# Input projection: seven-product K pairs in fewer column chunks

## The chip, the cores and the metric

The kernel runs on one core of a Trainium2 chip. The metric is the device time of one execution in microseconds (us), lower is better. The core's engines work side by side, each through its own queue in order: PE (TensorE, matrix products), DVE (VectorE), ACT (ScalarE), POOL (GpSimd), and SP, which here only issues transfers.

## The reference

Two layers, 256 tokens, width 2048, all in float32. Each layer projects the normed input to twelve chunks of 512 columns, runs two kinds of attention on them, projects back, and adds a feed-forward block:

```python
h = rms_norm(x, pre_mix_norm[l])
proj = h @ w_in[l]              # (256, 2048) @ (2048, 6144)
# q, k, v of stick-breaking attention: column chunks 0 to 5
# q, k, v of differential attention: column chunks 6 to 11
x = x + rms_norm(mix @ w_o[l], post_mix_norm[l])
x = x + rms_norm(swiglu(rms_norm(x, pre_ffn_norm[l])), post_ffn_norm[l])
```

## The kernel before

**Products.** Each float32 factor is split into a rounded part and a rest (`hi` and `lo` for weights, two halves of `xT` for the input), and one product is three matmuls: hi times hi, hi times lo, lo times hi. ACT makes `hi`, DVE the rest `lo` (line 369). A matmul has 128 x 128 stationary values (input or attention data) and 512 moving ones (weights).

**Input projection** (`mixer_in`). The twelve column chunks are done in six pairs of chunks, in the order of `PAIRS`: (6, 8), (10, 7), (9, 0), (11, 2), (1, 3), (4, 5). They are called the first to sixth pair here, `n` is 0 to 5. The 2048 rows of K form eight *K pairs* of two blocks of 128 rows. For one K pair, two column chunks and two halves of the tokens, the plain way (`eight_in`) takes eight products, 24 matmuls. The other way (`phased`) takes seven products, 21 matmuls, by a scheme of the Strassen kind: it multiplies sums of weight blocks by sums of token blocks. The second to sixth pair do K pairs 0 to 3 (`IN_SEVEN`) in seven products and 4 to 7 (`IN_PLAIN`) in eight; the first pair does all eight plainly.

**What seven products need.** Sums of the weights are made on the way. A transfer engine adds two blocks in DRAM ahead of time (`sums_ahead`: a copy at line 302 and an adding transfer at line 308, both issued by POOL, into `sum`), and SP loads that into half of a `raw` tile; where the sum isn't ready when the order is written, DVE makes it (line 378). DVE then forms three more sums per K pair (lines 380, 384, 399, on `u` and `raw`), and seven halves of a `hi`/`lo` pair are split instead of four. In `phased`, all K pairs' first four products (g0, t1, t2, t3) come first; then ACT copies the four banks into `w` (`kept_part`, line 1222), DVE combines three of them (lines 1253 to 1255), and then come g1, b22 and t4. `settle` adds `w` to the banks at the end of the pair (line 1266). Sums of the token blocks are formed once per layer and K pair, and serve all pairs of chunks: `sums_of`, with `fin`, `sin`, `shin`, `slin` as tiles, called in the first pair at K pairs 3 to 6 (layer 0) or 2 to 5 (layer 1).

**Attention.** Its steps stand among the projection's matmuls. A `tick` is counted for every two products, and generators continue after so many ticks: `flip` transposes q and k (`qkT_ps`), `diff_weights` makes scores `s_df`, their softmax `e_df` (ACT) and its transposes `pT_df`, `attend` the outputs `o_df`; `stick_weights` uses `za_sb` and `zb_sb`. `rotate` turns q and k on POOL (lines 984 to 987).

**Order and room.** A scheduler puts the instructions of each engine in order ahead of time and may move one past another that it doesn't depend on. `hi` and `lo` have six buffers each, `raw` has four, and `feed_jobs` prepares weights a few tiles ahead of PE.

Of the kernel before, what the change touches and what calls it, by code (L numbers as in the profile page):

```python
# [22 lines left out]
KT = D // P  # L23
# [13 lines left out]
O_SEVEN = (4, 5)  # L37
PAIRS = ((6, 8), (10, 7), (9, 0), (11, 2), (1, 3), (4, 5))
IN_SEVEN = (0, 1, 2, 3)
IN_PLAIN = (4, 5, 6, 7)  # L40
SEVEN = (2, 4, 5, 6)
FIRST_SEVEN = (6,)
FIRST_ORDER = (0, 1, 3, 2, 7, 4, 6, 5)
# [37 lines left out]
def weight_order():  # L81

    order = []

    def queue(*blocks):
        order.append(blocks)
        return len(order) - 1

    def queue_pair(name, l, kp, c):
        return queue((name, l, 2 * kp, c), (name, l, 2 * kp + 1, c))  # L90

    roles = {}

    def queue_phase(key, name, l, kps, cc):
        for a, b in zip(kps[::2], kps[1::2]):
            roles[queue(*((name, l, 2 * kp + 1, cc[1]) for kp in (a, b)))] = "u1", key, (a, b)
            for kp in (a, b):
                roles[queue(*((name, l, 2 * kp, c) for c in cc))] = "first", key, (kp,)
        for a, b in zip(kps[::2], kps[1::2]):
            roles[queue(*((name, l, 2 * kp + 1, cc[0]) for kp in (a, b)))] = "g1", key, (a, b)  # L100

    plan = []
    sevens, own = set(), set()
    for l in range(L):
        lay = {"in": {}, "o": {}, "gate": {}, "up": {}, "down": {}}
        for n, (ca, cb) in enumerate(PAIRS):
            if n:
                queue_phase(("in", l, n), "w_in", l, IN_SEVEN, (ca, cb))
            for kp in IN_PLAIN if n else range(KT // 2):
                lay["in"][ca, kp] = queue_pair("w_in", l, kp, ca)  # L110
                lay["in"][cb, kp] = queue_pair("w_in", l, kp, cb)
        queue_phase(("o", l), "w_o", l, KP_O[:2], (0, 1))
        order_o = [(c, kp) for kp in KP_O[2:] for c in (0, 1)]
        order_o += [(c, kp) for kp in LATE_O for c in (2, 3)] + [(c, kp) for c in (2, 3) for kp in LAST_O]
        lay["order_o"] = order_o
        for c, kp in order_o:
            lay["o"][c, kp] = queue_pair("w_o", l, kp, c)
            if c == 3 and kp in O_SEVEN:
                own.add(lay["o"][c, kp])
        for c in range(FF // CW):  # L120
            for kp in gate_order(c):
                lay["gate"][c, kp] = queue_pair("w_gate", l, kp, c)
                lay["up"][c, kp] = queue_pair("w_up", l, kp, c)
                if kp in gate_sevens(c):
                    sevens.add(lay["up"][c, kp])
        for half in range(2):
            cc = (2 * half, 2 * half + 1)
            order_d = [(c, kp) for kp in range(FF // P // 2) for c in cc]
            if half == 1 and l + 1 < L:
                order_d[-len(DOWN_LATE) :] = DOWN_LATE  # L130
            for c, kp in order_d:
                lay["down"][c, kp] = queue_pair("w_down", l, kp, c)
                if c % 2 and kp in DOWN_SEVEN[half]:
                    sevens.add(lay["down"][c, kp])
        plan.append(lay)
    return order, plan, sevens, own, roles
# [49 lines left out]
def kernel(  # L186
# [802 lines left out]
    def opening(pool, accs, xT, stats, sums_of, settle):  # L989

        xr = []

        def load():
            kp = len(xr)
            xr.append(pool.tile([P, 2, S], F32, tag="tok", name=f"xr{kp}"))
            nc.sync.dma_start(xr[kp], x_columns[:, 2 * kp : 2 * kp + 2, :])

        opened = []

        def split(k):  # L1000
            g, src = gains[:, k : k + 1], xr[k // 2][:, k % 2, :]
            if k == 0:
                with tc.high_priority(offset=URGENT):
                    opened.append(nc.vector.tensor_scalar(out=xT[k][:, 0, :], in0=src, scalar1=g, scalar2=None, op0=ALU.mult))
            else:
                nc.scalar.activation(xT[k][:, 0, :], src, AF.Copy, scale=g)
            nc.vector.scalar_tensor_tensor(
                out=xT[k][:, 1, :], in0=src, scalar=g, in1=xT[k][:, 0, :].bitcast(F32), op0=ALU.mult, op1=ALU.subtract
            )

        xr.append(pool.tile([P, 2, S], F32, tag="tok", name="xr0"))
        nc.scalar.dma_start(gains[:, 0:32], gain_columns[:, 0:32])
        nc.scalar.dma_start(xr[0][:, 0, :], x_columns[:, 0, :])
        nc.scalar.dma_start(xr[0][:, 1, :], x_columns[:, 1, :])
        both = []
        for i in range(2):
            both.append((
                wpool.tile([P, 2, CW], F32, tag="raw", bufs=4, name=f"raw{i}"),
                wpool.tile([P, 2, CW], F32R, tag="hi", bufs=6, name=f"hi{i}"),
                wpool.tile([P, 2, CW], F32R, tag="lo", bufs=6, name=f"lo{i}"),  # L1020
            ))
            raws.append(both[i][0])
        for kk in range(2):
            for i in range(2):
                loads.append(nc.sync.dma_start(raws[i][:, kk, :], stream[i][:, kk, :]))
        load()
        fetch(4)
        for kk in range(2):
            split(kk)
            for raw, hi, lo in both:  # L1030
                nc.scalar.activation(hi[:, kk, :], raw[:, kk, :], AF.Copy)  # L1031
                with tc.issue_after(opened[0].ins):
                    nc.vector.tensor_tensor(out=lo[:, kk, :], in0=raw[:, kk, :], in1=hi[:, kk, :].bitcast(F32), op=ALU.subtract)
        for i in range(2):
            ready[i] = both[i][1:]
        fed[0] = 2
        for kp in range(KT // 2):
            if kp:
                split(2 * kp)
                split(2 * kp + 1)  # L1040
            if kp + 2 < KT // 2:
                load()
                fetch(2 * kp + 6)
            for part in ((0,), (1,)) if kp == KT // 2 - 1 else (range(NT),):
                eight_in(accs, xT, 0, PAIRS[0], kp, part, kp == 0, kp == KT // 2 - 1, 0)
                if kp == KT // 2 - 1:
                    settle(part[0])
            if 3 <= kp < 7:
                next(stats)
            if 3 <= kp < 3 + len(IN_SEVEN):  # L1050
                sums_of(IN_SEVEN[kp - 3])

    def first_stats(pool, rs):
# [36 lines left out]
    def mixer_in(pool, l, rs, xT, mix, mixed, began):  # L1090
        heads = {}
        forms, forms_o = {}, {}
        mix_pool[0] = pool.sums

        def sums_of(kp):
            forms[kp] = pair_forms(pool, pool.sums, len(IN_SEVEN), xT, kp, f"in{l}")

        for n, cc in enumerate(PAIRS):
            banks = began[0] if n == 0 and began else four_banks(n == 0, [f"in{l}_{c}_{t}" for t in range(NT) for c in cc])
            alone = n == len(PAIRS) - 1  # L1100
            w, toks = None, {}
# [50 lines left out]
                opening(pool, banks, xT, first_stats(pool, rs), sums_of, settle)  # L1152
                start(lambdas())
            else:
                kps = IN_PLAIN if n else range(KT // 2)
                ahead = list(KP_O[:2]) if alone else []
                if n + 1 < len(PAIRS):
                    start(sums_ahead(("in", l, n + 1)))
# [2 lines left out]
                if n:  # L1161
                    open_sums[0] = True
                    w = pool.tile([P, 4, CW], F32, tag="gpost", bufs=1, name=f"w{l}_{n}")
                    w = [w[:, i, :] for i in range(4)]
                    phased(banks, forms, xT, ("in", l, n), IN_SEVEN, w)
                for j, kp in enumerate(kps):
                    last = j == len(kps) - 1
                    if n == 0 and 2 <= j < 2 + len(IN_SEVEN):
                        sums_of(IN_SEVEN[j - 2])
                    if n == 0 and 3 <= j < 7:  # L1170
                        put_away(f"in{l}", j - 3)
                    if n == 0 and j < 3:
                        continue
                    if n == 0 and j == 3:
                        for t in range(NT):
                            squares_of(t, pool, f"in{l}", began[1][t], (2, 3), began[2])
                        rs += [inv_rms(t, pool, f"in{l}", part=began[1][t]) for t in range(NT)]
                        scales(rs)
                    if last:
                        for t in range(NT):  # L1180
                            eight_in(banks, xT, l, cc, kp, (t,), False, last)
                            settle(t)
                    else:
                        eight_in(banks, xT, l, cc, kp, range(NT), False, last)
                    if ahead and heads[0, 1].keys() >= {"qdone", "kdone"}:
                        kp = ahead.pop(0)
                        forms_o[kp] = pair_forms(pool, pool, 4, mix, kp, f"o{l}", tags=("tok", "tok"))
# [241 lines left out]
    xT = None  # L1429
    for l in range(L):  # L1430

        pool = Rooms(tc, f"att{l}")
        if l == 0:
            xT = x_tiles("xT0")
# [49 lines left out]
        xT = x_tiles(f"xF{l}")  # L1484
# [331 lines left out]
```

## Time and profile before

| | |
|---|---|
| median of 3 runs | 2188.01 us (2187.4 to 2188.73) |
| profiled execution | 2187.7 us, its span 2186.0 us |
| granted TensorE clock | 0.999 |
| PE / DVE / ACT / POOL busy | 2160.5 / 2013.7 / 1459.2 / 310.2 us |
| the six pairs of layer 0 | from about 6 to 306 us |
| the six pairs of layer 1 | from about 1090 to 1393 us |

Times in the profile's rows count from the start of the span. In a row of a stretch, (x214) is the number of instructions and PEclk the share of full clock granted. In a row of the timeline stand the start, the duration, engine, line, operation, and written tile <- read tiles. A row of waits reads: engine, tile and line that waited <- what ended the wait: us in total, times, longest. Buffer numbers are left out of names.

### The profile page before, as it was taken

The page shows a single profiled execution, that of the slowest core. Times are in us where ns is not written, and L with a number is a line of the kernel's source. Part 1 is how long each engine was busy: PE and PEld are TensorE (multiplying, and loading weights), DVE is VectorE, ACT ScalarE, POOL GpSimd, SP SyncE. Part 2 cuts the span into 40 slices and gives each one's busy share as a digit, 9 for nine tenths or more (in the row PEclk, how much of TensorE's full clock was granted, in tenths as well). Part 3 has the DMA queues.
Part 4 walks back from the last instruction along what each step waited for, and adds up shares of the span by engine and source line. Part 5 has one row for each costly group of instructions (what it writes and reads, how often), then busy time and mean ns, then how long its engine had stood idle before and what let it go on. Part 6 is the DMA issues. An engine that isn't in the chain of part 4 may idle for free.

```text
span 2186.0 us, 29154 instructions
## 1 busy us (share of the span) xinstructions
PE 2160.5 (99%) x9872; PEld 1769.3 (81%) x9872; DVE 2013.7 (92%) x2784; ACT 1459.2 (67%) x2203; POOL 310.2 (14%) x318
## 2 busy tenths in 40 slices
PE   9999999999999999999999999999999999999998
PEld 7777888888888888888877778888888888888886
DVE  8998988899999999999898999878999999999997
ACT  7677876656666666666576777757666666676664
POOL 1321000022222220000023110000312212200000
PEclk9999999999999999999999999999999999999999
DMA  8667655587887776767477675655977878767673
GB/s 311 217 206 228 192 210 198 166 298 236 242 258 229 234 237 222 236 222 257 147 257 219 206 230 181 223 198 164 303 237 243 260 223 235 237 216 242 206 266 101
DMA packets 156743, 491.44 MB, mean 225 GB/s; under 512 B 18208, under 2 KB 19232, under 8 KB 155440
## 3 DMA queue, kind: packets, MB, share of 16 engines
q1 hardware_dynamic: 131376, 436.04, 56.7%
q0 software_dynamic: 24640, 53.00, 13.3%
q8 instruction: 77, 1.26, 0.2%
q14 instruction: 74, 0.61, 0.1%
q10 hardware_dynamic: 576, 0.54, 0.1%
HBM read 481.12 MB, written 29.36 MB: 234 GB/s over the span
## 4 chain that ended last, share of the span: by engine, by line
PE 83%; DVE 10%; DMA 3%; ACT 2%; issue 2%; SPq 0%; DVEq 0%; ACTq 0%
PE c L1345 21%; DVE lo L369 5%; PE dn L1665 4%; PE dn L1664 4%; PE dn L1667 4%; PE in L1288 4%; PE in L1287 4%; PE in L1289 4%; PE p L1288 3%; PE c L1288 3%; PE c L1287 3%; PE p L1289 3%; PE c L1289 3%; PE p L1287 3%; PE o L719 2%; PE o L717 2%
## 5 line engine op out<-in xcount | busy, mean ns | idle before, releaser
L369 DVE TENSOR_TENSOR lo<-raw,hi 128x1024 fp32r<-128x1024 f32 (+1 forms) x492 | 580.3, 1195 | 45.7 <-ACT hi L431 38.9
L431 ACT ACTIVATE hi<-raw 128x1024 fp32r<-128x1024 f32 x424 | 436.4, 1058 | 95.2 <-DMA raw<-in_weights_in_turn_dram 58.8
L1345 PE MATMUL c<-hi,xF 128*128 128x512 f32 x1344 | 364.5, 392 | 0.5 <-DVE xF L632 0.5
L1345 PEld LDWEIGHTS c<-hi,xF 128*128 128x128 f32 x1344 | 249.8, 188 | 53.0 <-ACT act L1551 1.4
L324 POOL DMA_DIRECT2D T<-in_weights_in_turn_dram x122 | 107.7, 882 | 1148.5 <-PE c L1345 319.1
L1345 PE MATMUL c<-lo,xF 128*128 128x512 f32 x672 | 207.4, 390 | 0.0
L345 ACT ACTIVATE Th<-T 128x512 fp32r<-128x512 f32 x122 | 77.2, 633 | 192.4 <-DVE T L356 191.3
L345 ACT ACTIVATE Th<-G 128x1024 fp32r<-128x1024 f32 x122 | 129.1, 1058 | 81.1 <-DVE G L357 80.0
L1664 PE MATMUL dn<-hi,jh 128*128 128x512 f32 x416 | 162.0, 389 | 0.0
L1665 PE MATMUL dn<-lo,jh 128*128 128x512 f32 x416 | 161.8, 389 | 0.0
L347 DVE TENSOR_TENSOR Tl<-G,Th 128x1024 fp32r<-128x1024 f32 x122 | 149.1, 1222 | 11.6 <-ACT Th L345 11.6
L347 DVE TENSOR_TENSOR lo<-T,hi 128x1024 fp32r<-128x1024 f32 x122 | 153.9, 1262 | 0.1
L357 DVE TENSOR_TENSOR G<-G,T 128x1024 f32<-128x1024 f32 x122 | 148.8, 1220 | 4.9 <-POOL lo L434 2.7
L431 ACT ACTIVATE hi<-G 128x1024 fp32r<-128x1024 f32 x122 | 129.0, 1057 | 36.3 <-DMA G<-in_weights_in_turn_dram 19.6
L1345 PEld LDWEIGHTS c<-lo,xF 128*128 128x128 f32 x672 | 126.0, 188 | 26.4
L345 ACT ACTIVATE hi<-T 128x1024 fp32r<-128x1024 f32 x122 | 128.1, 1050 | 12.4 <-PE c L1289 9.5
L369 DVE TENSOR_TENSOR lo<-G,hi 128x1024 fp32r<-128x1024 f32 x104 | 126.9, 1220 | 9.3 <-ACT hi L431 9.3
L1667 PE MATMUL dn<-hi,jl 128*128 128x512 f32 x416 | 128.1, 389 | 0.0
L1287 PE MATMUL in<-hi,xT 128*128 128x512 f32 x284 | 112.7, 402 | 0.7 <-ACT hi L1031 0.4
L1288 PE MATMUL in<-lo,xT 128*128 128x512 f32 x284 | 111.4, 393 | 0.2
L1289 PE MATMUL in<-hi,xT 128*128 128x512 f32 x284 | 111.0, 391 | 0.0
L1288 PE MATMUL in<-lo,xI 128*128 128x512 f32 x260 | 102.4, 394 | 4.0 <-DVE lo L369 4.0
(470 smaller groups left out, 5257.6 us busy)
## 6 DMA issues: line engine op xcount, KB each, us to landing
raw<-in_weights_in_turn_dram SPq DMA_DIRECT2D x468, 512.0 KB, 4.8
T<-in_weights_in_turn_dram SPq DMA_DIRECT2D x122, 512.0 KB, 5.1
G<-in_weights_in_turn_dram SPq DMA_DIRECT2D x122, 512.0 KB, 5.4
T<-in_weights_in_turn_dram POOLq DMA_DIRECT2D x122, 256.0 KB, 5.7
sum<-in_weights_in_turn_dram POOLq DMA_DIRECT2D x80, 256.0 KB, 5.0
u<-in_weights_in_turn_dram SPq DMA_DIRECT2D x44, 256.0 KB, 6.0
raw<-in_weights_in_turn_dram SPq DMA_DIRECT2D x34, 256.0 KB, 4.2
raw<-sum SPq DMA_DIRECT2D x30, 256.0 KB, 4.6
```

The costliest lines, as they stand in the source:

```text
L345: nc.scalar.activation(h, w, AF.Copy)
L347: newest_rest[i] = nc.vector.tensor_tensor(out=l, in0=w, in1=h.bitcast(F32), op=ALU.subtract)
L357: nc.vector.tensor_tensor(out=g, in0=g, in1=t2.unsqueeze(1).to_broadcast([P, 2, CW]), op=ALU.add)
L369: rests.append(nc.vector.tensor_tensor(out=lo, in0=src, in1=hi.bitcast(F32), op=ALU.subtract))
L431: nc.scalar.activation(hi, raw, AF.Copy)
L1287: nc.tensor.matmul(a, sh, hi, start=first, stop=False, skip_group_check=open_sums[0])
L1288: nc.tensor.matmul(a, sh, lo, start=False, stop=False, skip_group_check=open_sums[0])
L1289: newest_product[0] = nc.tensor.matmul(a, sl, hi, start=False, stop=last, skip_group_check=open_sums[0])
L1345: nc.tensor.matmul(a, stat[part], w[j][:, kk, :], start=first and kk + n == 0, stop=last and kk == 1 and n == 2)
L1664: nc.tensor.matmul(accs[c, t], sh, hi[:, kk, :], start=first, stop=False, skip_group_check=open_sums[0])
L1665: nc.tensor.matmul(accs[c, t], sh, lo[:, kk, :], start=False, stop=False, skip_group_check=open_sums[0])
L1667: nc.tensor.matmul(accs[c, t], sl, hi[:, kk, :], start=False, stop=last, skip_group_check=open_sums[0])
```

## The change

The constant set of K pairs becomes one for each pair of column chunks: none in the first, K pairs 0 and 1 in the second, third and fifth, 0 to 3 in the fourth and sixth. The token sums of K pairs 2 and 3 are now formed in the third pair, at its second and fourth plain K pair.

```diff
-IN_PLAIN = (4, 5, 6, 7)
+IN_SEVENS = ((), (0, 1), (0, 1), IN_SEVEN, (0, 1), IN_SEVEN)
+IN_PLAIN = tuple(tuple(kp for kp in range(8) if kp not in mine) for mine in IN_SEVENS)
+FORMS_AT = {(2, 1): 2, (2, 3): 3}
...
-                queue_phase(("in", l, n), "w_in", l, IN_SEVEN, (ca, cb))
-            for kp in IN_PLAIN if n else range(KT // 2):
+                queue_phase(("in", l, n), "w_in", l, IN_SEVENS[n], (ca, cb))
+            for kp in IN_PLAIN[n]:
...
-            if 3 <= kp < 3 + len(IN_SEVEN):
+            if 3 <= kp < 5:
                 sums_of(IN_SEVEN[kp - 3])
...
-                kps = IN_PLAIN if n else range(KT // 2)
+                kps = IN_PLAIN[n]
...
-                    phased(banks, forms, xT, ("in", l, n), IN_SEVEN, w)
+                    phased(banks, forms, xT, ("in", l, n), IN_SEVENS[n], w)
                 for j, kp in enumerate(kps):
                     last = j == len(kps) - 1
-                    if n == 0 and 2 <= j < 2 + len(IN_SEVEN):
+                    if n == 0 and 2 <= j < 4:
                         sums_of(IN_SEVEN[j - 2])
+                    if (n, j) in FORMS_AT:
+                        sums_of(FORMS_AT[n, j])
```

In the written order, DVE has 63 rows fewer, ACT 26, POOL 20 and SP 15; PE has 36 more matmuls.

DVE at the head of the second pair of layer 1, before. 409, 410, 412 and 413 are the weights of K pairs 0 to 3, `u1_...` their second blocks, 414 the first that the last three products of K pairs 0 and 1 need:

```order
L380 TENSOR_TENSOR u1_408_0_10591<-u1_408_0_10591,raw409_10595 128x512
L369 TENSOR_TENSOR lo409_0_10598<-raw409_10595,hi409_0_10597 128x1024
L384 TENSOR_TENSOR raw410_10636<-raw410_10636,u1_408_1_10593 128x512
L369 TENSOR_TENSOR lo410_1_10645<-u1_408_1_10593,hi410_1_10644 128x512
L380 TENSOR_TENSOR u1_411_0_10714<-u1_411_0_10714,raw412_10718 128x512
L369 TENSOR_TENSOR lo410_1_10645<-raw410_10636,hi410_1_10644 128x512
L380 TENSOR_TENSOR u1_411_1_10716<-u1_411_1_10716,first413_10741 128x512
L369 TENSOR_TENSOR lo412_0_10722<-raw412_10718,hi412_0_10721 128x1024
```

The same place now; 411 is what 414 was:

```order
L386 TENSOR_TENSOR raw410_10536<-raw410_10536,u1_408_1_10495 128x512
L401 TENSOR_TENSOR u1_408_1_10495<-raw411_10612,u1_408_1_10495 128x512
L371 TENSOR_TENSOR lo410_1_10545<-raw410_10536,hi410_1_10544 128x512
L371 TENSOR_TENSOR lo411_0_10615<-raw411_10612,hi411_0_10614 128x1024
L371 TENSOR_TENSOR lo411_1_10621<-u1_408_0_10493,hi411_1_10620 128x1024
L371 TENSOR_TENSOR lo411_2_10633<-u1_408_1_10495,hi411_2_10632 128x1024
L371 TENSOR_TENSOR lo412_10645<-raw412_10642,hi412_10644 128x1024
L1257 TENSOR_TENSOR w1_1_10611<-w1_1_10611 128x512
```

Where the sums and splits of two more K pairs stood, the last splits of the two that remain and the first plain split follow at once.

PE in the same pair, before, around the first transposes of q (`qkT_ps`), 70 projection matmuls into the pair:

```order
L1287 MATMUL in1_10_1_10711<-hi415_1_10824,xI0_5_9986 128x512
L1138 MATMUL qkT_ps1_6_0_10968<-ident_90,tok1_6_0_10664 128x128
L1288 MATMUL in1_10_0_10709<-lo415_0_10819,xI0_5_9986 128x512
L1289 MATMUL in1_10_0_10709<-hi415_0_10818,xI0_5_9986 128x512
L1287 MATMUL in1_10_0_10709<-hi415_0_10818,xI0_7_9988 128x512
```

Now, 120 projection matmuls into it:

```order
L1292 MATMUL in1_7_0_10608<-lo419_10752,xI0_10_9919 128x512
L1293 MATMUL in1_7_0_10608<-hi419_10751,xI0_10_9919 128x512
L1140 MATMUL qkT_ps1_6_0_10834<-ident_90,tok1_6_0_10563 128x128 x4
L1291 MATMUL in1_10_1_10609<-hi418_10745,xI0_10_9919 128x512
L1292 MATMUL in1_10_1_10609<-lo418_10746,xI0_10_9919 128x512
```

The transposes moved from among the last products of the seven-product part into the plain part. In layer 0 the first scores moved with them, from 61 matmuls into the pair to 168; in layer 1 they stood at 168 before.

DVE in the third pair of layer 1 now, with the token sums of K pair 2 among plain splits; no such rows stood there before:

```order
L1089 TENSOR_TENSOR fin1_2_11188<-xI0_5_9914 128x256
L1301 TENSOR_TENSOR sin1_2_11191<-fin1_2_11188 128x128
L1299 TENSOR_TENSOR sin1_2_11191<-fin1_2_11188 128x128
L371 TENSOR_TENSOR lo434_11203<-raw434_11200,hi434_11202 128x1024
L1300 TENSOR_TENSOR sin1_2_11191<-sin1_2_11191,fin1_2_11188 128x128
L371 TENSOR_TENSOR lo435_11209<-raw435_11206,hi435_11208 128x1024
```

The sums came here from the end of the first pair.

## The prediction

> **What bounds the kernel now.** I read the page first, then the busy times of the ten pairs of column chunks that the change can reach, then who the PE waited for in each.
>
> ```profile
> PE 2160.5 (99%) x9872; PEld 1769.3 (81%) x9872; DVE 2013.7 (92%) x2784; ACT 1459.2 (67%) x2203; POOL 310.2 (14%) x318
> ```
>
> PE and DVE are both nearly full over the span, so an exchange of work between them has to be judged stage by stage. The next rows are the second to sixth pair of column chunks, of layer 0 (first five) and layer 1 (last five): length, then busy time of each engine with its instructions.
>
> ```profile
> core 0: us, PE busy (x) PEld busy (x) DVE busy (x) ACT busy (x) POOL busy (x), PEclk, DMA share, GB/s
> 50.60:100.20 49.60, 48.01 (x214) 36.34 (x213) 46.35 (x65) 31.12 (x43) 15.43 (x22) 1.00 0.76 242
> 100.20:153.50 53.30, 51.21 (x245) 40.10 (x244) 48.91 (x87) 39.39 (x95) 18.16 (x20) 1.00 0.64 198
> 153.50:198.70 45.20, 44.90 (x217) 36.44 (x216) 39.06 (x52) 29.80 (x48) 8.24 (x13) 1.00 0.73 233
> 198.70:255.60 56.90, 54.61 (x271) 43.43 (x271) 52.41 (x91) 45.33 (x98) 5.48 (x8) 1.00 0.60 186
> 255.60:306.30 50.70, 50.70 (x251) 42.39 (x250) 47.68 (x72) 41.42 (x63) 2.74 (x4) 1.00 0.55 175
> 1138.10:1187.80 49.70, 45.55 (x213) 35.82 (x212) 43.58 (x50) 31.30 (x41) 17.84 (x24) 1.00 0.72 222
> 1187.80:1241.70 53.90, 51.64 (x245) 40.36 (x244) 50.42 (x90) 40.40 (x96) 11.56 (x20) 1.00 0.64 195
> 1241.70:1286.90 45.20, 44.91 (x217) 36.53 (x216) 40.67 (x55) 31.26 (x50) 8.30 (x13) 1.00 0.74 233
> 1286.90:1342.10 55.20, 53.90 (x272) 43.60 (x271) 50.80 (x88) 44.32 (x95) 5.38 (x8) 1.00 0.63 192
> 1342.10:1392.80 50.70, 50.70 (x251) 42.39 (x250) 47.78 (x72) 41.51 (x63) 2.74 (x4) 1.00 0.56 176
> ```
>
> All ten have 180 projection matmuls. The second pair has nearly the same number of instructions as the fourth (213 or 214 against 217) and takes 49.6 and 49.7 us against 45.2 in both layers: some 4.5 us in each second pair are not matmul work. The third and fifth hold more attention matmuls and cannot be compared so.
>
> What a matmul costs where nothing waits is its spacing. These are the first and the last of 68 consecutive matmuls of the second pair:
>
> ```profile
> 80.93 0.39 PE L1287 MATMUL in<-hi,xT 128*128 128x512 f32 x1
> 96.11 0.39 PE L1288 MATMUL in<-lo,xT 128*128 128x512 f32 x1
> ```
>
> (96.11 - 80.93) / 67 = 0.227 us, though a row lasts 0.39. So a stall that shows as idle g costs g + 0.16 us, since the row before it covers the first 0.39 - 0.23 us.
>
> [...]
>
> Who ended PE's idle time (us, times, longest), in order: second, third, fourth, fifth pair of layer 0, then second, third and fifth of layer 1 (its fourth repeats the 0.3 row; the sixth pairs have none):
>
> ```profile
> PE in L1287 <- ACT hi L386: 1.2, 3, 0.5
> PE in L1287 <- ACT hi L379: 0.2, 1, 0.2
> PE in L1288 <- DVE lo L369: 1.2, 1, 1.2
> PE o_df L849 <- ACT pT L968: 0.8, 1, 0.8
> PE in L1288 <- DVE lo L369: 0.3, 1, 0.3
> PE za_sb L867 <- ACT e_df L943: 0.8, 1, 0.8
> PE o_df L849 <- ACT pT L968: 0.5, 1, 0.5
> PE pT_df L962 <- ACT e_df L943: 0.5, 1, 0.5
> PE qkT_ps L1138 <- ACT kT L1139: 0.2, 1, 0.2
> PE in L1287 <- DVE w L1266: 0.2, 1, 0.2
> PE in L1288 <- DVE lo L369: 4.2, 5, 1.4
> PE in L1288 <- DVE lo L369: 1.3, 2, 0.9
> PE s_df L927 <- ACT e_df L943: 0.6, 1, 0.6
> PE in L1287 <- DVE w L1266: 0.4, 1, 0.4
> PE za_sb L867 <- ACT e_df L943: 0.8, 1, 0.8
> PE o_df L849 <- ACT pT L968: 0.4, 1, 0.4
> ```
>
> With 0.16 us added each time, waits for the weights' splits (lo, hi, and w of the settling) cost 2.0, 1.4 and 0.4 us in the second, third and fifth pair of layer 0, and 5.0, 2.2 and 0 in layer 1: 11.0 us. Waits for the attention's ScalarE steps cost 1.0 and 2.6 us in the third and fifth pair of layer 0, 0.8 and 1.5 in layer 1: 5.9 us. The fourth pairs lose 0.5 each. These are the whole prize, with one addition: the second pair of layer 0 is 4.9 us above a stall-free fourth (45.2 - 0.5 = 44.7), 2.9 more than its listed waits; these are starts too little late to show as idle.
>
> **The change, priced.** Per layer it turns two K pairs of the second, third and fifth pair from seven products into eight: 12 K pairs in all.
>
> PE, added: 24 instead of 21 matmuls each, 12 x 3 x 0.227 = 8.2 us, or 1.4 us for each of the six pairs of column chunks. All of it is on the path, because PE is the engine that never rests where it isn't made to wait.
>
> DVE, removed: prices are spacings between starts.
>
> ```profile
> 1135.75 1.22 DVE L369 TENSOR_TENSOR lo<-raw,hi 128x1024 fp32r<-128x1024 f32 x1
> 1136.89 0.69 DVE L369 TENSOR_TENSOR lo<-u,hi 128x512 fp32r<-128x512 f32 x1
> 1137.49 0.69 DVE L384 TENSOR_TENSOR raw<-raw,u 128x512 f32<-128x512 f32 x1
> ```
>
> A 1024-wide split takes 1.14, a 512-wide operation 0.60. A phased K pair needs three half-width sums (1.80), two half-width splits (1.20) and two and a half full ones (2.85): 5.85 us, against 4.77 us of matmuls (21 x 0.227). A plain one needs two splits, 2.28 us against 5.45 us. Each K pair turned takes 3.57 us off DVE, 12 of them 42.8; three sums (L378) that were made on DVE for want of a ready one go too, 1.8. By itself this is worth nothing; it is worth what PE waits less. ACT loses 24 half-width and a net 6 full-width splits, and is no bound in any row (at most 45.33 of 56.90). POOL loses 20 of its 80 `sum` transfers, SP 12 half loads of `u1` and 18 into halves of `raw`, against 15 more whole ones; DMA is at 0.76 or less in these rows, so I price that at nothing, and if it uncovers a gain it is DVE's waits for pre-made sums, below.
>
> DVE, moved: the token sums of K pairs 2 and 3 leave the first pair for the third.
>
> ```profile
> 1128.44 0.75 DVE L1087 TENSOR_TENSOR fin<-xI 128x256 f32<-128x256 f32 x2
> 1129.11 0.28 DVE L1297 TENSOR_TENSOR sin<-fin 128x128 f32<-128x128 f32 x1
> 1129.31 0.68 DVE L1306 TENSOR_TENSOR slin<-sin,shin 128x512 fp32r<-128x512 f32 x1
> ```
>
> One set is 0.67 + 4 x 0.20 + 0.60 = 2.07 us, so 4.1 us come into each third pair, where 7.1 leave: DVE is still relieved by 3.0 there, and the sums stand among plain K pairs, whose splits leave 3.2 us in each. That cover hides them; without it they would cost up to 8.3 us in the two layers. The first pair ends with DVE 4.1 us earlier, so the splits for the second can begin sooner, as far as the loads are there: DVE's waits for them are a row of their own (us, times).
>
> ```profile
>   DVE u L380: 9.8, 9
> ```
>
> Pair by pair, against 44.7 us plus 1.4 for the added matmuls: the second pairs could come to 46.1, which is 3.5 and 3.6 us less. I leave 0.5 us of waits in each, because the burst of two K pairs still meets the rotations of q and k on POOL, in which a half-width split takes longer:
>
> ```profile
> 1142.44 0.95 DVE L369 TENSOR_TENSOR lo<-raw,hi 128x512 fp32r<-128x512 f32 x1
> 1142.80 0.77 POOL L985 TENSOR_TENSOR rb<-tok,rope_sb 128x64 f32<-128x64 f32 x1
> ```
>
> That gives -3.0 and -3.1. (0.95 against 0.69 is 0.26 us. [...])
>
> Third pairs: +1.4 each, of 1.4 and 2.2 us of split waits I take 1.3 and 1.8 back (part of the settling wait stays). In layer 0 the first softmax scores move from among the second pair to its end, as they already stand in layer 1, whose third pair is 0.6 us longer; I add 0.5. So +0.6 and -0.4. Fifth pairs: +1.4 each; of the waits (0.4 and 2.6; 1.5) I take 1.0 and 0.4 back, since DVE and ACT answer sooner: +0.4 and +1.0. Fourth pairs, with an emptier DVE before them: -0.3 each. First and sixth pairs, output projection and feed-forward: nothing.
>
> Sum: -3.0 - 3.1 + 0.6 - 0.4 + 0.4 + 1.0 - 0.6 = -5.1 us. The profiled execution took 2187.7 us (span 2186.0), 0.3 under the median of the runs, 2188.0; the sum is put on the median: 2182.9 us. Bounds of what comes back: nothing, +8.2; every wait named, 11.0 + 5.9 + 1.0 + 2.9 = 20.8, so -12.6. I stand nearer the good end because the fourth and sixth pairs carry four phased K pairs and wait 0.5 us or not at all: two should fit in nearly everywhere.
>
> **Rivals.** *The waits stay at the head of the pair (slower).* DVE's arrears over a burst of two K pairs are 11.7 + 1.8 (three sums on w) - 9.5 = 4.0 us, over four 23.4 + 1.8 - 19.1 = 6.1: they fall by a third alone. If the waits fall likewise, a third of 11.0 + 2.9 comes back, 4.6 us, and the time is 2188.0 + 8.2 - 4.6 = 2191.6. Against it: in 80.93 to 96.11 us PE runs without a wait right after its burst, so DVE makes up arrears fast, and the sixth pairs wait for nothing. It is slower than before from less than 8.2 us recovered, measurably from less than 3.8.
>
> *All slack returns.* -12.6 gives 2175.4; needs the attention waits to go as well, though what stands around them in the order hardly changes. Decides from 12.6 us recovered.
>
> *The waits move on.* PE, freed from the splits, reaches the attention's steps sooner in relation to ScalarE, and waits of the e_df and pT kind grow: half of the 13.3 us recovered is lost again, 2188.0 + 8.2 - 6.7 = 2189.5; with a quarter lost 2186.2. I take 2187. For it: these waits exist in four of the six pairs. Against: most steps stand as many matmuls apart as before.
>
> **How the numbers follow.** Forecast 0.48 (2180 to 2186), all slack 0.22, waits move on 0.18, waits stay 0.12. No change is what lies within 0.2% (4.4 us): 2183.6 to 2192.4. The forecast's range lies 0.6 below that edge, so faster is 0.22 + 0.48 x 0.6 = 0.51; slower takes half of the last case, 0.06; the rest, 0.43, is the same. The range 2177 to 2190 leaves out half of the second case's reach and the upper half of the last.
>
> **What would show it.** Second pairs of about 46.5 us with under 1 us of idle before `in` matmuls; third 53.9 and 53.5, fifth 57.3 and 56.2; 36 more `in` matmuls at the same spacing; DVE busy about 45 us less; first pairs no shorter. Second pairs above 48 us would make the prediction wrong, as would new waits of `in` matmuls in the third pair where its sums stand.

## The result and the profile after

The changed kernel took 2190.56 us (median of 20 runs, 2186.68 to 2194.13), the kernel before on the same chip 2186.53 (20 runs). The ratio is 1.0019, 95% interval 1.0012 to 1.0026: 4.2 us slower (2.6 to 5.7), where 5.1 us faster was forecast. The profiled execution took 2189.47 us, its span 2187.4. The span of before's profiled execution was 2186.0: the two traces differ by 1.4 us, which the rows below account for together with the fourth pairs, 0.6 shorter in all. The other 2.8 of the 4.2 us lie between executions, and no trace here shows where.

The page's first part, to be set beside the same line of before:

```profile
PE 2165.4 (99%) x9908; PEld 1779.1 (81%) x9908; DVE 1975.3 (90%) x2715; ACT 1439.7 (66%) x2173; POOL 291.8 (13%) x298
```

PE has the 36 matmuls more. DVE is busy 38.4 us less, with 69 instructions fewer. The stretches of the second, third, fifth and sixth pair of layer 0, then of layer 1, by the columns used in the prediction:

```profile
50.80:98.10 47.30, 46.51 (x220) 36.98 (x219) 38.12 (x52) 28.16 (x42) 11.27 (x16) 1.00 0.67 218
98.10:151.40 53.30, 52.14 (x251) 41.70 (x250) 47.22 (x93) 37.77 (x88) 11.68 (x20) 1.00 0.64 207
195.90:256.80 60.90, 57.52 (x284) 47.22 (x284) 46.69 (x84) 42.39 (x89) 5.79 (x9) 0.97 0.60 195
256.80:306.60 49.80, 49.80 (x247) 41.63 (x246) 46.29 (x67) 40.08 (x59) 2.33 (x4) 1.00 0.53 169
1138.80:1185.10 46.30, 45.99 (x220) 37.25 (x219) 33.48 (x37) 26.97 (x39) 15.81 (x19) 1.00 0.65 213
1185.10:1239.40 54.30, 52.08 (x251) 41.68 (x250) 46.18 (x91) 36.59 (x87) 10.63 (x20) 1.00 0.64 202
1284.70:1345.00 60.30, 57.23 (x283) 47.13 (x282) 46.68 (x84) 42.05 (x89) 5.79 (x9) 0.97 0.62 197
1345.00:1394.80 49.80, 49.80 (x246) 41.62 (x245) 46.32 (x67) 40.08 (x59) 2.29 (x4) 1.00 0.55 169
```

The second pairs came down by 2.3 and 3.4 us. The fifth went up by 4.0 and 5.1; 0.9 of that is attention work that used to stand in the sixth, so the two together are 3.1 and 4.2 us longer. These are also the only rows here in which the granted clock is below 1.00. Who ended PE's idle time in the second, then in the fifth pair, layer 0 and layer 1 in turn:

```profile
PE in L1292 <- DVE lo L371: 0.8, 1, 0.8
PE in L1292 <- DVE lo L371: 0.3, 1, 0.3
PE o_df L851 <- ACT pT L970: 3.4, 2, 3.0
PE o_df L851 <- ACT pT L970: 3.1, 1, 3.1
```

The waits for the weights' splits went as forecast. A wait of 3 us stands in their place, three pairs later, at the output products of attention, for ScalarE's copy of the transposed softmax (`pT`, line 970). ScalarE's timeline there, layer 0:

```profile
214.62 1.06 ACT L433 ACTIVATE hi<-raw 128x1024 fp32r<-128x1024 f32 x1 [0.94 <-PE in L1293]
218.74 1.06 ACT L433 ACTIVATE hi<-raw 128x1024 fp32r<-128x1024 f32 x1 [3.06 <-DMA raw<-in_weights_in_turn_dram]
219.70 0.57 ACT L970 COPY pT<-pT_df 128x512 f32<-128x512 f32 x1
```

ScalarE is not busy, it is stuck: for 3.06 us it waits for a load, at the split of a weight tile (number 75 in layer 0, so `hi75<-raw75`) that PE needs only later. The copy that PE needs at once stands behind it in the queue. The load is this one, issued between 210.2 and 210.3:

```profile
raw<-in_weights_in_turn_dram SPq DMA_DIRECT2D x1, 512.0 KB, 8.4
```

8.4 us, where the page of the profile has 4.9 as the median of the kernel's 484 such loads.

On PE's timeline the copy's input, the transposes `pT_df`, was done 4 us before the copy began, and PE, back at work, is slow for a while:

```profile
215.11 0.60 PE L964 MATMUL pT_df<-ident,e_df 128*128 128x128 f32 x4
...
220.32 0.49 PE L851 MATMUL o_df<-v,pT 128*128 128x128 f32 x2 [3.00 <-ACT pT L970]
...
222.69 0.63 PE L1292 MATMUL in<-lo,xT 128*128 128x512 f32 x1
223.11 0.63 PE L1293 MATMUL in<-hi,xT 128*128 128x512 f32 x1
...
224.53 0.40 PE L1291 MATMUL in<-hi,xT 128*128 128x512 f32 x1
224.76 0.40 PE L1292 MATMUL in<-lo,xT 128*128 128x512 f32 x1
```

From 222.69 to 223.11 is 0.42 us for a 512-wide matmul that takes 0.23 from 224.53 on.

The same place in the kernel before, on PE and on ScalarE:

```profile
220.56 0.60 PE L962 MATMUL pT_df<-ident,e_df 128*128 128x128 f32 x4
222.38 0.38 PE L848 MATMUL o_df<-v,pT 128*128 128x128 f32 x2
...
224.73 0.49 PE L849 MATMUL o_df<-v,pT 128*128 128x128 f32 x2
```

```profile
224.01 0.67 ACT L968 COPY pT<-pT_df 128x512 f32<-128x512 f32 x1
```

The copy was not early there either: it began 3.4 us after the transposes began, against 4.6 now. But eight projection matmuls stood between the first output product, which doesn't need this copy, and the second, which does (222.51 to 224.22 us, left out here); now the second follows the first at once. In both layers that is 2.1 us of cover lost on PE, and the copy is done some 1.1 us later behind its transposes. Together they are the 3.2 us by which the output products come late (the idle time, and the 0.16 us that the matmul before it covers).

### The profile page after: what moved, and what is told of

It is laid out like the page before. It is cut to its first block, busy times and chain, and to the rows that moved or that the text cites. A ratio compares the mean times of both kernels' runs of the same rounds, so it can differ in the third digit from the quotient of the medians.

```text
span 2187.4 us, 29021 instructions
## 1 busy us (share of the span) xinstructions
PE 2165.4 (99%) x9908; PEld 1779.1 (81%) x9908; DVE 1975.3 (90%) x2715; ACT 1439.7 (66%) x2173; POOL 291.8 (13%) x298
## 5 line engine op out<-in xcount | busy, mean ns | idle before, releaser
L371 DVE TENSOR_TENSOR lo<-raw,hi 128x1024 fp32r<-128x1024 f32 (+1 forms) x498 | 592.7, 1206 | 71.5 <-ACT hi L433 57.1
L433 ACT ACTIVATE hi<-raw 128x1024 fp32r<-128x1024 f32 x448 | 459.7, 1059 | 120.6 <-DMA raw<-in_weights_in_turn_dram 70.9
L349 DVE TENSOR_TENSOR Tl<-G,Th 128x1024 fp32r<-128x1024 f32 x122 | 149.2, 1223 | 11.6 <-ACT Th L347 11.6
L1291 PE MATMUL in<-hi,xT 128*128 128x512 f32 x314 | 125.2, 401 | 0.5 <-DVE xT L1006 0.5
L1292 PE MATMUL in<-lo,xT 128*128 128x512 f32 x314 | 123.2, 393 | 1.1 <-DVE lo L371 1.1
L1293 PE MATMUL in<-hi,xT 128*128 128x512 f32 x314 | 122.8, 392 | 0.0
L1291 PE MATMUL in<-hi,xI 128*128 128x512 f32 x290 | 116.7, 402 | 0.5 <-ACT w L1226 0.5
```

Source lines behind the costliest of these rows:

```text
L349: newest_rest[i] = nc.vector.tensor_tensor(out=l, in0=w, in1=h.bitcast(F32), op=ALU.subtract)
L371: rests.append(nc.vector.tensor_tensor(out=lo, in0=src, in1=hi.bitcast(F32), op=ALU.subtract))
L433: nc.scalar.activation(hi, raw, AF.Copy)
L1291: nc.tensor.matmul(a, sh, hi, start=first, stop=False, skip_group_check=open_sums[0])
L1292: nc.tensor.matmul(a, sh, lo, start=False, stop=False, skip_group_check=open_sums[0])
L1293: newest_product[0] = nc.tensor.matmul(a, sl, hi, start=False, stop=last, skip_group_check=open_sums[0])
```

## Experiments

Each was timed against the kernel before on the same chip; the differences in us are the ratio and its interval times before's median of 2186 to 2187, and need not be the difference of two medians. Theory 1: the fifth pairs lost their time because the copy `pT` stood in ScalarE's queue behind a split whose load landed late.

### Which part of the change carries the loss

**The fifth pair alone.**

```diff
-IN_SEVENS = ((), (0, 1), (0, 1), IN_SEVEN, (0, 1), IN_SEVEN)
-FORMS_AT = {(2, 1): 2, (2, 3): 3}
+IN_SEVENS = ((), IN_SEVEN, IN_SEVEN, IN_SEVEN, (0, 1), IN_SEVEN)
+FORMS_AT = {}
...  # the first pair forms the token sums of all four K pairs again
```

> The change in the fifth pair alone: second and third pairs as in the kernel before, all forms in the first pair. The split hi75 stands ahead of the copy pT on ScalarE, as in the changed kernel. Theory 1: the wait of about 3 us at L851 is there in both layers, the fifth pairs take 59.5 to 61 us, and the kernel is 5 to 9 us slower than the kernel before. Rival E (the wait comes only with the earlier start of the fifth pair or with the forms' time in the third): no wait over 1 us at L851, fifth pairs longer by the forecast's 0.4 and 1.0 us alone, and the kernel is within 2 us of before.

2195.36 us, 7.9 slower than before (5.2 to 10.3). The wait is there without the rest of the change, in layer 0 and in layer 1:

```profile
PE o_df L851 <- ACT pT L970: 4.5, 1, 4.5
PE o_df L851 <- ACT pT L970: 2.7, 2, 2.6
```

The fifth pairs took 61.9 and 58.6 us, one above and one under the 59.5 to 61 expected: the wait was longer in layer 0, and in layer 1 the clock stayed whole (1.00 over the 4 us behind the wait). Rival E falls: the moved forms are not needed for the wait, nor is an earlier start, since this fifth pair of layer 1 began 1.8 us later than before.

**Second and third pair alone.**

```diff
-IN_SEVENS = ((), (0, 1), (0, 1), IN_SEVEN, (0, 1), IN_SEVEN)
+IN_SEVENS = ((), (0, 1), (0, 1), IN_SEVEN, IN_SEVEN, IN_SEVEN)
```

> The change in the second and third pairs alone: the fifth pair keeps its four phased K pairs. On ScalarE the copy pT stands ahead of hi75, as in the kernel before. Theory 1: the second pairs keep their gains (47.3 and 46.3 us), the third stay at 53.3 and 54.3, the fifth go back to 56.9 and 55.2 or a little less, and no wait over 1 us stands at L851 there: 4 to 7 us faster than the kernel before. Rival D (whatever the second pairs gain is given back at the next place where TensorE waits for a softmax): the fifth pairs are longer than before by 2 us or more also here, and the kernel is within 3 us of before.

2184.58 us, 2.8 faster (1.1 to 4.8). Second pairs 47.4 and 45.9 us, fifth 55.2 and 55.5, and no wait over 0.6 us at L851 there. The direction is theory 1's; the size is under its 4 to 7. The third pair of layer 1 took 55.5 where 54.3 was expected, which is part of it.

**The second pair alone.**

```diff
-IN_SEVENS = ((), (0, 1), (0, 1), IN_SEVEN, (0, 1), IN_SEVEN)
-FORMS_AT = {(2, 1): 2, (2, 3): 3}
+IN_SEVENS = ((), (0, 1), IN_SEVEN, IN_SEVEN, IN_SEVEN, IN_SEVEN)
+FORMS_AT = {}
...  # as above
```

> The change in the second pair alone: two phased K pairs there, four in all later pairs, all forms in the first pair. Theory 1: second pairs 47.3 and 46.3 us, third and fifth pairs as in the kernel before or a little shorter, no wait over 1.2 us in the fifth: 4 to 7 us faster than the kernel before. Rival D (what the second pair gains is partly given back at the waits for softmax in the third and fifth): third pairs longer than 53.4 and 53.9 us by 1 us or more, and the kernel is only 1 to 3 us faster than before, as it was with second and third changed.

2186.36 us, 0.7 slower (1.3 faster to 2.4 slower): a miss, and not for the third pair's softmax that rival D named. The gain is lost where the second pair hands over to the third, by a wait of 1.5 us in layer 0 and 3.9 in layer 1. Layer 1, the waits around 1186:

```profile
PE in L1291 <- ACT v L1116: 3.9, 1, 3.9
```

The copy that frees one of the pair's banks (`v`, in `settle`) stands on ScalarE behind a split for the third pair's four phased K pairs, which waits for a sum on DVE:

```profile
1184.96 0.63 ACT L388 ACTIVATE hi<-raw 128x512 fp32r<-128x512 f32 x1 [1.98 <-DVE raw L386]
1185.49 0.67 ACT L1116 ACTIVATE v<-in,rs_in 128x512 f32<-128x512 f32 x1
```

**Second and third pair, the forms left in the first.**

```diff
-IN_SEVENS = ((), (0, 1), (0, 1), IN_SEVEN, (0, 1), IN_SEVEN)
-FORMS_AT = {(2, 1): 2, (2, 3): 3}
+IN_SEVENS = ((), (0, 1), (0, 1), IN_SEVEN, IN_SEVEN, IN_SEVEN)
+FORMS_AT = {}
...  # as above
```

> The change in the second and third pairs alone, and the forms of all four K pairs in the first pair as in the kernel before. Theory J (the forms that were moved into the third pair cost time there, since VectorE is what TensorE waits for at pT_df): third pairs 0.5 to 1.5 us shorter than the 53.4 and 55.5 us of the same kernel with two forms in the third pair, first pairs no longer than before, and the kernel is 1 to 3 us faster than that one, 4 to 6 us faster than before. Rival K (the forms only change places): first pairs longer by what the third pairs lose, and the kernel is 2 to 3 us faster than before, as it was.

2189.29 us, 2.8 slower (0.4 to 5.2), where theory J said faster. It has the plan of K pairs of the kernel that was 2.8 faster; only the two forms' place differs. In the third pair of layer 1 (2.9 us in layer 0):

```profile
PE pT_df L964 <- DVE e_df L955: 3.7, 1, 3.7
```

Here it is DVE's queue: the softmax's last steps (lines 952 to 955) stand behind the rest of a split that waits for its `hi`, and ScalarE waited for that tile's load.

```profile
1210.21 1.23 DVE L371 TENSOR_TENSOR lo<-raw,hi 128x1024 fp32r<-128x1024 f32 x1 [2.61 <-ACT hi L433]
1211.35 0.22 DVE L952 TENSOR_SCALAR sm_df<-sm_df,lam 128x2 f32<-128x2 f32 x1
```

So taking the forms out of the third pair gains nothing: its two pairs took 56.3 and 58.3 us without them, 53.4 and 55.5 with them. That they keep DVE from reaching such splits ahead of the softmax is my reading; no run tests it alone. Theory J falls, rival K too.

### The order on ScalarE

**The fifth pair's splits recorded later.**

```diff
-                        eight_in(banks, xT, l, cc, kp, range(NT), False, last)
+                        eight_in(banks, xT, l, cc, kp, range(NT), False, last, LOOKAHEAD - (2 if n == 4 else 0))
```

> The changed kernel, with the weights' splits of the fifth pair recorded two jobs less ahead. TensorE's order is that of the changed kernel to the row; on ScalarE the copy pT (L970) of the first two df heads now stands ahead of the split hi75 instead of behind it. Theory 1 (the fifth pairs lost their time because the copy pT stood in ScalarE's queue behind a split whose load landed late): TensorE's wait of 3.0 and 3.1 us before L851 falls under 1 us in both layers, the slow matmuls right behind it go too, the fifth pairs come down from 60.8/60.3 us to 55.5 to 57.5, and the kernel is 7 to 10 us faster than the changed one, about 5 us faster than the kernel before. Rival A (the load itself is too late, whoever stands behind it): the wait only moves some matmuls on, to the in matmuls that read hi75, and 2 to 3 us per layer stay: within 2 us of the changed kernel. Rival B (the splits have no cover in the fifth pair with two jobs less ahead): a wait at L1291 of over 1 us per K pair, slower than the changed kernel.

2183.48 us, 2.6 faster than before (0.9 to 4.6), so about 6.8 faster than the changed kernel, just under the 7 to 10 expected. PE's order is the same, without the eight matmuls of cover; who stands in front of whom on ScalarE differs. Waits in the fifth pair of layer 0:

```profile
PE o_df L851 <- ACT pT L970: 0.7, 2, 0.4
```

In layer 1 they are 1.5 with a longest of 1.0. The fifth pairs took 56.6 and 57.4 us, clock 1.00. The load was no earlier: the split began at 220.12 us, against 218.74 in the changed kernel, and ScalarE still waited 2.00 us for it, now behind the copy:

```profile
217.56 0.57 ACT L970 COPY pT<-pT_df 128x512 f32<-128x512 f32 x1
220.12 1.06 ACT L433 ACTIVATE hi<-raw 128x1024 fp32r<-128x1024 f32 x1 [2.00 <-DMA raw<-in_weights_in_turn_dram]
```

PE waits for no split in either fifth pair. Rivals A and B fall.

**The output products later on PE.**

```diff
             attending[0] += 1
+            if (kind, g, hp) == ("df", 1, 0):
+                yield 4
```

> The changed kernel, with the output products o_df of the first two df heads of the second group (L851 and around) recorded four ticks later: some 30 matmuls, about 6.5 us at 0.227 us, later on TensorE. The split hi75 still stands ahead of the copy pT on ScalarE. Theory 1: TensorE has other work until the copy is done, so the wait of 3.0 and 3.1 us at L851 is gone, and the kernel is 7 to 10 us faster than the changed one. Rival A (the late load): the wait goes to the in matmuls that read hi75, at most 2 us better than the changed kernel. Rival C (the pair is short of ScalarE and VectorE time as a whole, the wait at L851 is only where it shows): a wait of about the same size appears at the next step of attention in the pair, and the time stays within 2 us of the changed kernel.

2187.22 us, level with before (1.7 faster to 2.0 slower), so about 4 faster than the changed kernel: half of what was expected. The wait at L851 is gone, but in layer 0 this one came:

```profile
PE za_sb L898 <- ACT ah_sb L891: 1.3, 1, 1.3
```

`ah_sb` is the next step behind the same stuck split. So work on PE between the copy's transposes and the products that need them hides the late copy too, as the eight matmuls did in the kernel before. The profiled fifth pairs were 58.0 and 56.7 us, which would give more than the median shows; the profiled execution, 2184.05 us, was the fastest of this kernel's.

### Why the load was late

**The pre-made sums later.** While raw75 was on its way (210.2 to 218.7), the view of the transfers gives the queue of SP and that of POOL these shares of the 16 DMA engines, over 100% together:

```profile
q1 hardware_dynamic: 580, 1.89, 59.2%
q0 software_dynamic: 375, 0.67, 44.6%
```

POOL's part comes from the last of the eight transfers, four copies and four that add, which make the sums of weight blocks in DRAM for the sixth pair.

```diff
-                    start(sums_ahead(("in", l, n + 1)))
+                    start(sums_ahead(("in", l, n + 1)), 12 if n == 4 else 1)
```

> The changed kernel, with GpSimd's eight transfers that form the sums for the sixth pair begun 12 ticks later, about 20 us, so that they no longer run while raw74 to raw76 are loaded. TensorE's order is that of the changed kernel, and hi75 still stands ahead of the copy pT. Theory H (these transfers make the load of raw75 late): raw75 lands within 6 us of its issue instead of 8.4, the wait at L851 falls to 1 us or less, and the kernel is 6 to 10 us faster than the changed one. Rival I (the loads and the split products' u loads hold each other up, since buffers come free in a bunch): raw75 still takes 7 us or more, the wait stays at 2.5 us or more, and the time is within 2 us of the changed kernel.

2182.01 us, 4.4 faster than before (2.4 to 6.1), 8.6 faster than the changed kernel. The same split load, now issued at 211.1:

```profile
raw<-in_weights_in_turn_dram SPq DMA_DIRECT2D x1, 512.0 KB, 3.5
```

3.5 us instead of 8.4. On ScalarE the split still stands ahead of the copy, but waits for nothing; TensorE's wait at that place is gone and the fifth pairs are 57.0 and 57.7 us at full clock:

```profile
196.80:253.80 57.00, 55.67 (x283) 45.81 (x282) 46.83 (x85) 41.90 (x89) 5.75 (x9) 1.00 0.67 207
1282.60:1340.30 57.70, 55.68 (x284) 45.84 (x283) 46.83 (x85) 42.01 (x89) 5.87 (x9) 1.00 0.67 205
```

Rival I falls. What remains is a wait of 1.3 and 2.0 us for the next two heads' copy, 30 us later.

**The same delay in the kernel before.** Same edit, on the kernel before.

> The kernel before, with GpSimd's eight transfers for the sixth pair begun 12 ticks later, as it was done to the changed kernel. Theory H (the delay is worth something only because it takes the late load away from in front of the copy pT): in the kernel before the copy pT stands ahead of the split, so there is nothing to win: within 2 us of the kernel before, fifth pairs 56 to 57 and 55 to 56 us. Rival M (the delay is worth 5 us or so by itself, and the change nothing): 3 to 6 us faster than the kernel before, fifth pairs shorter by 2 us or more.

2185.75 us, 0.2 faster (2.2 faster to 1.7 slower): the delay is worth nothing there. Late loads were no novelty (the one issued at 212.84 took 7.1 us in the kernel before); what was new is that ScalarE stood waiting for one ahead of the copy, with no cover on PE. Rival M falls.

### What the wait does to the clock

**Filler in the wait.**

```diff
-                nc.tensor.matmul(o0, w[0], v[:, 0, cols], start=True, stop=True)
+                for _ in range(15 if (kind, g, hp, j) == ("df", 1, 0, 0) else 1):
+                    nc.tensor.matmul(o0, w[0], v[:, 0, cols], start=True, stop=True)
```

> The changed kernel, with the first output product of o_df of the second group's first two df heads issued 15 times instead of once, each with the same operands into the same columns: 14 more matmuls of about 0.11 us, 1.5 us, which read the part of pT that is long there. They stand right ahead of the matmul that waits 3.0 and 3.1 us for the copy pT, so TensorE idles about 1.5 us instead, and the copy itself comes no earlier. Theory F (an idle time of some 3 us lowers TensorE's clock for what follows): the waiting matmul starts at the same distance from the pair's start, but the matmuls behind it stand 0.11 and 0.23 us apart from the first on, the fifth pairs come down by 1.5 to 2 us each (60.8 and 60.3 to about 59), and the kernel is 3 to 4 us faster than the changed one, about level with the kernel before. Rival G (the slow matmuls come from something that the other engines do at that moment): spacing of 0.21 and 0.43 us stays, and the time is that of the changed kernel within 1.5 us.

2193.3 us, 6.8 slower than before (4.6 to 9.0): the time is a miss, and so are the fifth pairs, 62.2 and 62.8 us instead of about 59. Each of these float32 matmuls is two records of 0.11 us, so the filler took 3.3 us, not 1.5, and covered the wait whole in layer 0 and all but 0.5 us of it in layer 1; and a second wait, of 1.9 and 1.8 us, then stood at the next two heads' copy, in layer 0 with a clock of 0.59 over the 4 us behind it. The clock is what the run is for. Stretches (PEclk is the third number from the end): of the changed kernel, the wait and the 4 us behind it; of this kernel, the same place, then the second wait and the 4 us behind it.

```profile
216.90:220.30 3.40, 0.42 (x3) 0.19 (x1) 0.51 (x2) 1.56 (x3) 0.00 (x0) 1.00 1.05 350
220.30:224.30 4.00, 3.98 (x16) 3.55 (x17) 1.94 (x4) 2.36 (x11) 0.00 (x0) 0.57 0.97 359
```

```profile
221.00:225.00 4.00, 4.00 (x25) 3.52 (x24) 2.59 (x7) 2.33 (x11) 0.00 (x0) 1.00 1.04 405
249.00:251.00 2.00, 0.16 (x2) 0.00 (x0) 1.91 (x2) 1.99 (x4) 0.00 (x0) 1.00 0.48 184
251.00:255.00 4.00, 3.96 (x16) 3.48 (x17) 2.82 (x5) 2.05 (x9) 0.00 (x0) 0.59 0.04 10
```

With PE kept at work the same matmuls, beside the same work of ScalarE and the same loads, run at full clock (1.00 against 0.57), and behind the second wait PE ran at 0.59. Rival G falls: the slow matmuls belong to the idle time.

### What is to be had once nothing waits

**Both delays and the smaller plans.** Four kernels, the changed one or the one without the fifth pair's change, with the sums later in the fifth pair (12 ticks) or also in the second to fourth (8 ticks: `12 if n == 4 else 8 if n else 1`).

> The change in the second and third pairs alone, with the transfers for the sixth pair begun 12 ticks later. Theory H: no long wait stood in the fifth pair of this kernel without the delay (0.75 and 0.94 us were the longest), so the delay brings little: fifth pairs 55 to 56 us, the kernel 3 to 6 us faster than before, within 2 us of the changed kernel with the same delay. Rival M (the delay helps every plan of the fifth pair alike): 6 to 8 us faster than before.

2183.04 us, 3.5 faster than before (1.5 to 5.2), within the expectation: the delay adds little where the copy stood ahead and PE had its cover.

> The changed kernel, with the transfers for the sixth pair begun 12 ticks later, and those for the third to fifth pairs eight ticks later. If the transfers make loads late in the second to fourth pairs too (theory H, extended), the waits of 1 to 2 us in the third pairs at pT_df (L964) and o_df fall, third pairs come to 52.5 to 53.5 us, and the kernel is 6 to 8 us faster than before. Rival N (in these pairs the transfers are ready too late when they begin later, or they collide with the next loads): a wait on a sum at the head of the next pair, second to fourth pairs longer by 1 us or more, and at most 4 us faster than before.

2176.31 us, 8.5 faster (5.7 to 11.6): the change as it is, and with transfers out of the way the fastest kernel of the study. The third pairs:

```profile
97.60:149.20 51.60, 51.57 (x251) 41.73 (x250) 46.93 (x93) 37.69 (x89) 10.61 (x20) 1.00 0.66 215
1177.50:1229.50 52.00, 51.64 (x251) 41.70 (x250) 47.63 (x93) 38.10 (x89) 11.50 (x20) 1.00 0.66 215
```

They are 1.7 and 2.3 us shorter than in the changed kernel, and under the 52.5 to 53.5 expected. Rival N falls for this plan.

> The change in the second and third pairs alone, with the transfers for the sixth pair begun 12 ticks later and those for the third to fifth pairs eight ticks later. Theory H, extended: as the run before it, 5 to 8 us faster than the kernel before. Rival N: at most 3 us faster than before, with a wait on a sum at the head of a pair.

2188.45 us, 2.0 slower (0.0 to 3.7), as rival N said. At the head of the fifth pair of layer 0 stands this wait (3.2 us in layer 1):

```profile
PE in L1291 <- ACT v L1116: 4.4, 1, 4.4
```

It is for ScalarE's `v`, but behind a late sum: ahead of it, from 180 to 199 us, ScalarE waits for the load of a pre-made one, and DVE for 3.0 us (3.7 and 2.9 in layer 1):

```profile
ACT hi L381 <- DMA raw<-sum: 3.9, 1, 3.9
```

DVE's sums, the softmax that waits for DVE, and the copy `v` follow behind that. In the same kernel without delays, ScalarE has no such wait there.

**The delay in third and fifth pair only**, `{2: 8, 4: 12}.get(n, 1)`, in the kernel before and without the fifth pair's change.

> The kernel before, with the transfers that form sums begun eight ticks later in the third pair and 12 ticks later in the fifth. Theory P (the plain K pairs of the second pair are needed for the gain, since TensorE waits for VectorE's lo in the kernel before, not for a load): third pairs at most 1.5 us shorter than 53.4 and 53.9, second pairs as before, 49.6 and 49.7, and the kernel within 3 us of the kernel before. A wait at the head of the fourth pair on late sums can come on top, since four K pairs' sums are to be made. Rival M (the transfers' time alone): third pairs at 51.5 to 52 us, 4 to 6 us faster than before.

2191.27 us, 7.0 slower (4.2 to 9.6). In the third pair of layer 0 a new wait stands (2.3 in layer 1), and the second pairs still wait for splits:

```profile
PE oT_ps_df L819 <- DVE on_df L803: 2.5, 1, 2.5
```

`on_df` stands in DVE's queue behind sums and splits of phased K pairs. So the transfers' time alone is no gain, and rival M falls once more. Theory P is borne out in that, and missed the size: it said within 3 us of the kernel before, with third pairs at most 1.5 us shorter; they became longer, 55.9 and 56.7 us.

> The change in the second and third pairs alone, with the transfers begun eight ticks later in the third pair and 12 ticks later in the fifth; those of the fourth pair, which made the fifth wait 4.5 and 3.3 us when they too were later, at their old time. If the plain K pairs of the fifth pair cost their matmuls once nothing waits there: third pairs 51.6 and 52.0 us, fifth and sixth pairs together 105 to 106 us instead of 107.0 and 106.2, no wait over 1.5 us, 10 to 13 us faster than the kernel before and so 1 to 3 us faster than the changed kernel with all its transfers later. If the fifth pair's four phased K pairs bring other waits back: within 1 us of that kernel or slower.

2177.11 us, 8.1 faster (5.2 to 10.9), not to be told from the fastest, and under the 10 to 13 that the first case gave. Fifth and sixth pairs together are 105.3 and 106.1 us, against 106.9 and 106.3 there, but the second pair of layer 1 is 1.9 longer, where one wait of 1.3 us came. Once nothing waits, the fifth pair's plain K pairs are neither gain nor loss that can be measured.

## Why the prediction was wrong

**Second pairs: right.** -3.0 and -3.1 were forecast, -2.3 and -3.4 measured; the waits for `lo` fell to 0.8 and 0.3.

**Third and fourth pairs: right in sum.** Third +0.6 and -0.4, measured 0.0 and +0.4; fourth -0.3 each, measured -0.7 and +0.1. First pairs 44.6 and 48.0, no shorter, as written. These terms and the second pairs' come to -5.9; forecast was -6.5.

**Fifth pairs: the step that failed.** Forecast +0.4 and +1.0, "since DVE and ACT answer sooner"; measured, with the sixth, +3.1 and +4.2, where a wait of 3.0 and 3.1 us and the slow clock behind it (1.7 us) make some 4.7 a layer. Two things came together. ACT answered later: with two plain K pairs more, a whole-tile split whose load was still on its way stood in front of a copy that PE waits for. And PE asked sooner: the eight matmuls ahead of the product that needs the copy were gone. Each has a run that undoes it alone (the splits later, the output products later), and in each the wait of 3 us at that place is gone but for 1.0 us at most. Taking the late load away gave 4.4 us faster than before (2.4 to 6.1), and the 5.1 forecast lies in that interval.

**Two sentences carried the error.** "DMA is at 0.76 or less in these rows, so I price that at nothing": a mean over 50 us hid 8.5 us in which the two queues' shares add up to 104%. "What stands around them in the order hardly changes", and in the next rival "most steps stand as many matmuls apart as before", was said of the attention steps. On PE it was wrong for this one, by eight matmuls; on ScalarE I had not asked what the step in front of the copy waits for.

**The rival that came nearest** is "the waits move on". It names the right kind of wait and too small a price, because it took growth in proportion to what PE recovers, and this wait is set by a transfer and by the matmuls that were left to cover it. "The waits stay at the head of the pair" has the measured time nearly right (4.2 us slower against 3.6) by a mechanism that did not happen. "All slack returns" did not come true, but with the transfers moved 8.5 of its 12.6 us were had.

**DVE** lost 38.4 us, not about 45. Nothing hangs on it, and I did not look for the rest.

## What to carry to other kernels

In a queue that keeps its order, ask of every step that moves not only when it is needed but what it waits for: a short step that the bounding engine needs at once must not stand behind a step whose load is still on its way (here ScalarE waited 3.06 us for the load, and PE 3.00 for the copy). Count, too, what the bounding engine has to do between giving the work out and needing the answer: that cover can go when work is moved (here eight matmuls). Price transfers from the microseconds around a load, with all queues' shares added, and not from a stage's mean (here 104% over 8.5 us against 60% over the fifth pair). Where a plan removes work and the time does not fall, look for the next in-order queue before giving up the plan: here moving some transfers by up to 20 us turned 4.2 us slower into 8.5 faster.

## What the runs showed of the hardware

Behind the waits of 3.0 and 3.1 us in the changed kernel TensorE ran at a granted clock of 0.50 for 3.4 us: matmuls stood 0.43 us apart instead of 0.23, which adds 1.7 us to the wait. The two stretches:

```profile
220.75:224.16 3.41, 3.41 (x14) 3.02 (x13) 1.42 (x3) 1.86 (x11) 0.00 (x0) 0.50 0.98 360
1309.61:1313.02 3.41, 3.41 (x14) 3.02 (x13) 1.40 (x3) 1.88 (x11) 0.00 (x0) 0.50 0.99 345
```

Other waits were followed by slow matmuls too. Behind the wait of 4.5 us in layer 0 of the kernel with the fifth pair alone they stood 0.43 us apart. Behind the wait of 3.9 us in layer 1 of the kernel with the second pair alone the clock was 0.50 over 5.2 us, and behind the one of 1.9 us in layer 0 of the kernel with filler 0.59 over 4 us. But behind the wait of 2.6 us in layer 1 of the kernel with the fifth pair alone it was 1.00. The wait, then the 4 us behind it:

```profile
1309.80:1312.60 2.80, 0.25 (x3) 0.05 (x1) 0.48 (x1) 1.57 (x3) 0.00 (x0) 1.00 1.06 335
1312.60:1316.60 4.00, 3.99 (x22) 3.48 (x23) 2.59 (x7) 2.35 (x11) 0.00 (x0) 1.00 1.05 397
```

So the length of the wait alone does not decide: one of 1.9 us was followed by a slow clock, one of 2.6 us was not. No run shows what sets the two apart. In the kernel with filler, where PE was at work in place of the first wait, the clock was 1.00 over the next 4 us, against 0.57 in the changed kernel.
